# Head norms of q and k moved ahead of the gates' chain in a two-block transformer kernel

## The chip, the cores and the metric

The kernel runs on one core of one Trainium2 chip. The metric is device time in microseconds (us) of one execution. The core has five engines that work from queues of their own, each strictly in the order in which its instructions stand: TensorE (PE, with its weight loads PEld), VectorE (DVE), ScalarE (ACT), GpSimd (POOL) and SyncE (SP), which here only issues DMAs. They wait for each other through semaphores.

## The reference

256 tokens of width 1024 pass through two blocks in float32. The first block has a gated-delta layer and an HGRN2 layer. The second, where the change lies, is a mixer of three kinds of attention heads of width 64, followed by a feed-forward part:

```python
def _rms(x, g=None):                       # over one head's 64 columns
    xf = x.astype(jnp.float32)
    y = xf * lax.rsqrt(jnp.mean(xf * xf, axis=-1, keepdims=True) + EPS)
    return y if g is None else y * g.astype(jnp.float32)

def _mixer(hn, w_in, ...):
    proj = (hn @ w_in).astype(jnp.float32)
    fq, fk, fv, ff, mq, mk, mv, mi, mf, mo, bq, bk, bv = jnp.split(proj, idx, axis=-1)
    y_fox = _fox_attention(_rms(_to_heads(fq, 6), fox_q_g), _rms(_to_heads(fk, 6), fox_k_g),
                           _to_heads(fv, 6), ff + fox_f_bias)     # softmax with forget gates
    ...
    h_ml = _mlstm(mq, mk, mv, mi + ml_i_bias, mf + ml_f_bias)     # 4 heads with gates
    ...
    y_moba = _moba_attention(_rms(_to_heads(bq, 6), moba_q_g), _rms(_to_heads(bk, 6), moba_k_g),
                             _to_heads(bv, 6), slopes)            # softmax, 6 heads
    return concatenate([y_fox, y_ml, y_moba])
```

The "head norm" is `_rms` on the 24 q and k heads of the fox and moba kinds. The "gates" are `ff`, `mi` and `mf`: 14 columns per token, through a softplus and sums over the tokens.

## The kernel before

Every large product is made of three TensorE products of split float32 numbers (`hi*xh`, `hi*xl`, `lo*xh`). The weights come in one stream of 1 MB chunks; ACT casts each half chunk (`hi`), DVE forms the rest (`lo`, L206). Four half chunks of `hi` and `lo` have room, so a cast waits until TensorE has done with the half chunk four earlier. Results go to PSUM banks: four for the large products (tag `d`, in rows `psd`) and four for small ones (tag `m`, in rows `psm`), each used in turn and waited for by whoever needs it again.

The mixer (L1053) runs in this order on TensorE. `lstm_in` makes the mLSTM inputs and, beside the last of them, the gates' 16 columns. `heads` (L1139) then makes the q and k columns in three groups `g` of 512 columns, each for two halves `a_` of 128 tokens: 8 steps of 2 x 3 products, 48 products of 128x512 per group, in two `psd` banks. After each group two `head_norm` generators are queued. Then come the v columns in two groups of the same size (the `for g in range(2)` of `mixer`), then the output product.

Between the products small work is woven in. `Side` (L101) holds queues of generators; each has a width, the number of generators that may be under way. `side.tick(0.65)` after some products moves a planner's clock; a generator runs to its next `yield t` and is taken up again when the clock has moved by `t`. So the numbers behind `yield` are a plan, written as estimates, and they fix where TensorE's small products stand among the large ones: TensorE's instructions keep the order of the program. Those of ACT, DVE, POOL are put in order by a scheduler when the program is built. Three queues matter here:

- `gt`, width 1: `attention_gates`. After the softplus it makes `ag_cs` (sums over tokens, L1113), `ag_r` (L304), has TensorE transpose `ag_r`, copies and scans the result (`ag_rr`, `ag_mx`, L1126 and L1127), has it transposed back (`ag_mxc`), and sets `self.gated`.
- `kq`, width 2: `head_norm` (L1151). ACT squares the bank (`sq`), DVE sums 64 columns at a time (`hss`, L1158) and scales (L310), POOL raises to -1/2 (`hrs`, L321), DVE multiplies the bank by it (`sq`, L304), TensorE transposes four blocks into a `psm` bank, ACT and DVE copy them into `kq`. The multiplication is the last reader of the `psd` bank.
- `at`, width 4: `softmax_pair`, a pair of heads each. It waits for both norms of its group (pairs 0 and 1 need group 0, pairs 2 and 3 group 1, pairs 4 and 5 group 2). For each head of pairs 0 to 2 it takes a `psm` bank for the bias (two transposes of `ag_cs`) and one for the scores; heads of pairs 3 to 5 have their bias from POOL and take a score bank only. DVE frees them: two additions for the bias (with an ACT copy between them), two reductions for the scores (L1206, `pr`). All pairs are queued after the last q and k product.

Of the kernel before, what the change touches and what calls it, by code (L numbers as in the profile page):

```python
# [182 lines left out]
class Net:  # L183
# [966 lines left out]

    def head_norm(self, g, a_, b, kq):  # L1151
        nc, ep = self.nc, self.ep
        yield from self.wait(lambda: self.gated)
        sq = ep.tile([P, 512], F32, tag="sq", bufs=2, name=self.nm("sq"))
        ss, rs = (ep.tile([P, 8], F32, tag=n, bufs=2, name=self.nm(n)) for n in ("hss", "hrs"))
        v8 = lambda t: t.rearrange("p (h d) -> p h d", d=64)
        self.act(sq, b, AF.Square)
        nc.vector.tensor_reduce(ss, v8(sq), AX.X, ALU.add)  # L1158
        self.ts(ss, ss, 1.0 / 64, 1e-6)
        self.rsqrt(rs, ss)  # L1160
        self.tt(v8(sq), v8(b), rs.unsqueeze(2).to_broadcast([P, 8, 64]))
        yield 8.45
        t = self.ps("m")
        for j in range(4):
            self.tr(t[:, j * P:(j + 1) * P], sq[:, j * P:(j + 1) * P])
        s = slice(a_ * P, (a_ + 1) * P)
        for j in range(2):
            n = QK_BLOCKS[4 * g + j]
            self.act(kq[:, n, s], t[:, j * P:(j + 1) * P], AF.Copy, scale=self.gain[:, n // 3:n // 3 + 1])
        n = QK_BLOCKS[4 * g + 2]  # L1170
        m = QK_BLOCKS[4 * g + 3]
        nc.vector.tensor_copy(kq[:, n, s], t[:, 2 * P:3 * P])
        nc.vector.tensor_copy(kq[:, m, s], t[:, 3 * P:])
        self.kqdone.add((g, a_))
# [283 lines left out]
```

## Time and profile before

| what | us |
|---|---|
| median of 3 runs | 1015.01 (1011.16 to 1016.71) |
| the profiled execution | 1009.7 |
| its span in the trace | 1007.9 |
| TensorE busy | 979.7 (97%) |
| DVE busy | 757.2 (75%) |
| ACT busy | 555.2 (55%) |
| POOL busy | 51.2 (5%) |
| granted TensorE clock, mean | 0.998 |

The part that the change touches runs from 694.8 us (first q and k product) to 769.6 us (first product of the softmax weights with v). TensorE is busy nearly throughout; a busy share of TensorE counts the time in which it has a product under way, and its idle time is told with the engine it waited for. A row of the timeline gives the start, the duration, the engine, the line, the operation and its tiles, and in brackets the idle time of the engine before it.

### The profile page before, as it was taken

How to read it: one execution, taken by the hardware profiler on the slowest of the kernel's cores; microseconds unless marked ns; L12 is line 12 of the kernel's file. 1: busy time of each engine (PE TensorE's matmuls, PEld its weight loads, DVE VectorE, ACT ScalarE, POOL GpSimd, SP SyncE). 2: the span in 40 equal slices, each digit the busy share in tenths (PEclk: the TensorE clock that was granted, in tenths of full speed). 3: DMA queues.
4: the chain of work that ended last, by engine and by line, in shares of the span. 5: the costliest groups of instructions: out<-in, count | busy, mean ns of one | idle time of the engine just before them, and what ended most of it. 6: DMA issues, size and time to landing. Idle time of an engine off the chain costs nothing.

```text
span 1007.9 us, 19087 instructions
## 1 busy us (share of the span) xinstructions
PE 979.7 (97%) x7622; PEld 937.2 (93%) x7622; DVE 757.2 (75%) x1449; ACT 555.2 (55%) x1104; POOL 51.2 (5%) x59
## 2 busy tenths in 40 slices
PE   7999999999999999999999999899999999999998
PEld 5999989999998999998999999898867999999998
DVE  5788767878668978979697996879776787665543
ACT  6765556654544664464545544577566674444431
POOL 1000000000000000000000000000141000000000
PEclk9999999999999999999999999999999999999999
DMA  7445523345555685655556455354523257654560
GB/s 283 144 152 175 171 86 126 130 169 175 218 192 206 227 325 201 219 178 182 190 192 220 169 178 199 126 178 133 194 91 126 104 191 271 218 200 169 183 214 22
DMA packets 34617, 179.52 MB, mean 178 GB/s; under 512 B 7648, under 2 KB 8672, under 8 KB 16608
## 3 DMA queue, kind: packets, MB, share of 16 engines
q1 hardware_dynamic: 34096, 177.71, 49.9%
q8 instruction: 60, 0.98, 0.4%
q10 hardware_dynamic: 432, 0.59, 0.2%
q14 instruction: 29, 0.24, 0.1%
HBM read 176.97 MB, written 1.31 MB: 177 GB/s over the span
## 4 chain that ended last, share of the span: by engine, by line
PE 57%; DVE 7%; issue 4%; ACT 1%; POOL 1%; POOLq 0%; ACTq 0%; DVEq 0%
PE psd L294 49%; PE psm L294 6%; PE psm L297 2%; DVE lo L206 2%; DVE q L304 1%; ACT hi L206 1%; DVE xl L313 1%; DVE mt L313 0%; DVE wa L971 0%; DVE k L304 0%; DVE x L304 0%; DVE at L304 0%; DVE yl L217 0%; POOL hrs L321 0%; DVE lacc L313 0%
## 5 line engine op out<-in xcount | busy, mean ns | idle before, releaser
L206 DVE TENSOR_TENSOR lo<-raw,hi 128x1024 fp32r<-128x1024 f32 x280 | 341.2, 1222 | 132.4 <-ACT hi L206 130.2
L206 ACT CAST hi<-raw 128x1024 fp32r<-128x1024 f32 x280 | 292.9, 1047 | 249.1 <-PE psd L294 236.2
L294 PE MATMUL psd<-xh,hi 128*128 128x256 f32 (+1 forms) x1296 | 375.6, 290 | 0.0
L294 PE MATMUL psd<-xl,hi 128*128 128x256 f32 (+1 forms) x1296 | 366.8, 283 | 0.8 <-DVE xl L313 0.6
L294 PE MATMUL psd<-xh,lo 128*128 128x256 f32 (+1 forms) x1296 | 366.4, 283 | 0.2 <-DVE lo L206 0.2
L294 PEld LDWEIGHTS psd<-xl,hi 128*128 128x128 f32 x1296 | 245.7, 190 | 1.6 <-DVE xl L313 1.2
L294 PEld LDWEIGHTS psd<-xh,hi 128*128 128x128 f32 x1296 | 245.3, 189 | 1.0
L294 PEld LDWEIGHTS psd<-xh,lo 128*128 128x128 f32 x1296 | 245.5, 189 | 0.5 <-DVE lo L206 0.5
L294 PE MATMUL psd<-yh,hi 128*128 128x256 f32 x448 | 131.9, 294 | 3.7 <-ACT yh L216 3.7
L294 PE MATMUL psd<-yl,hi 128*128 128x256 f32 x448 | 127.1, 284 | 1.4 <-DVE yl L217 1.3
L294 PE MATMUL psd<-yh,lo 128*128 128x256 f32 x448 | 127.2, 284 | 0.0
L294 PEld LDWEIGHTS psd<-yh,hi 128*128 128x128 f32 x448 | 85.2, 190 | 5.2 <-ACT yh L216 4.3
L294 PEld LDWEIGHTS psd<-yl,hi 128*128 128x128 f32 x448 | 85.6, 191 | 2.4 <-DVE yl L217 2.4
L294 PEld LDWEIGHTS psd<-yh,lo 128*128 128x128 f32 x448 | 84.9, 189 | 0.1
L294 PE MATMUL psd<-hi,xh 128*128 128x512 f32 x144 | 59.0, 410 | 2.3 <-DVE sq L304 2.1
L971 DVE SCALAR_TENSOR_TENSOR wa<-wa,cr 128x1024 f32<-128x1024 f32 x48 | 58.4, 1218 | 2.8 <-ACT cr L316 1.6
L294 PE MATMUL psd<-hi,xl 128*128 128x512 f32 x144 | 56.9, 395 | 0.0
L294 PE MATMUL psd<-lo,xh 128*128 128x512 f32 x144 | 56.9, 395 | 0.0
L294 PE MATMUL psd<-al,hi 128*128 128x256 f32 x176 | 49.8, 283 | 0.0
L294 PE MATMUL psd<-ah,lo 128*128 128x256 f32 x176 | 49.7, 282 | 0.0
L294 PE MATMUL psd<-ah,hi 128*128 128x256 f32 x176 | 49.3, 280 | 0.0
L313 DVE SCALAR_TENSOR_TENSOR t<-psd,prm,t 128x255 f32<-128x255 f32 (+2 forms) x72 | 34.2, 476 | 3.9 <-ACT t L316 3.1
(330 smaller groups left out, 1381.9 us busy)
## 6 DMA issues: line engine op xcount, KB each, us to landing
raw<-in_w_dram SPq DMA_DIRECT2D x140, 1024.0 KB, 4.8
wa<-in_w_ada_dram SPq DMA_DIRECT2D x48, 512.0 KB, 4.8
cr<-in_c_dram SPq DMA_DIRECT2D x3, 512.0 KB, 6.0
out_dram<-fo SPq DMA_DIRECT2D x3, 256.0 KB, 2.1
cst<-in_cst_dram SPq DMA_DIRECT2D x1, 580.0 KB, 8.4
x<-in_xT_dram ACTq DMA_DIRECT2D x2, 256.0 KB, 4.4
x<-in_xT_dram SPq DMA_DIRECT2D x2, 256.0 KB, 5.0
lev<-in_lev_dram SPq DMA_DIRECT2D x1, 508.0 KB, 5.1
```

What stands on the lines that cost most here:

```text
L206: i = [nc.scalar.copy(hi, r), nc.vector.tensor_tensor(lo, r, hi.bitcast(F32), ALU.subtract)]
L294: self.nc.tensor.matmul(out, lhsT, rhs, start=start, stop=stop, skip_group_check=True, **k)
L297: self.nc.tensor.transpose(out, in_, self.c("ident")[:in_.shape[0], :in_.shape[0]])
L304: self.nc.vector.tensor_tensor(out, a, b, op)
L313: self.nc.vector.scalar_tensor_tensor(out, a, s, b, op0, op1)
L971: self.tc.keep_in_program_order(nc.vector.scalar_tensor_tensor(w, w, 1.0, c, ALU.mult, ALU.mult, accum_out=self.md(j)[:, i % 8:i % 8 + 1]))
```

## The change

In `head_norm` the wait for `self.gated` is moved from the first line to a place behind the multiplication, ahead of the transposes. The planner's delay between the multiplication and the transposes is 5.5 for one half of the tokens and 6.5 for the other, where it was 8.45 for both.

```diff
     def head_norm(self, g, a_, b, kq):
         nc, ep = self.nc, self.ep
-        yield from self.wait(lambda: self.gated)
         sq = ep.tile([P, 512], F32, tag="sq", bufs=2, name=self.nm("sq"))
...
         self.tt(v8(sq), v8(b), rs.unsqueeze(2).to_broadcast([P, 8, 64]))
-        yield 8.45
+        yield 5.5 + a_
+        yield from self.wait(lambda: self.gated)
         t = self.ps("m")
         for j in range(4):
             self.tr(t[:, j * P:(j + 1) * P], sq[:, j * P:(j + 1) * P])
```

What it does to the order shows at three places. The first is DVE at the norm of group 0, where the gates' chain runs too (`hss`, `hrs`, `sq` are the norm's; `ag_cs`, `ag_r` the gates').

```order
-L1158 TENSOR_REDUCE hss_8493<-sq_8492 128x8
-L1113 COPY ag_cs<-psm_8432 128x20
-L310 TENSOR_SCALAR hss_8493<-hss_8493 128x8
-L1158 TENSOR_REDUCE hss_8501<-sq_8500 128x8
+L1157 TENSOR_REDUCE hss_8424<-sq_8423 128x8
+L1157 TENSOR_REDUCE hss_8432<-sq_8431 128x8
+L310 TENSOR_SCALAR hss_8424<-hss_8424 128x8
+L1113 COPY ag_cs<-psm_8448 128x20
+L310 TENSOR_SCALAR hss_8432<-hss_8432 128x8
+L304 TENSOR_TENSOR sq_8423<-psd_8283,hrs_8425 128x512
+L304 TENSOR_TENSOR sq_8431<-psd_8284,hrs_8433 128x512
 L304 TENSOR_TENSOR ag_r<-ag_g,ag_cs 128x8
```

Both multiplications of the norm, each of which needs a result of POOL, now stand ahead of `ag_r`; before, `ag_r` stood ahead of both.

The second place is TensorE at the start of the v columns. Before, bias and score of two heads (the first of pairs 0 and 1) stood between the first products of v:

```order
L297 MATMUL psm_8640<-cst,ag_cs 128x128 x2
L294 MATMUL psm_8646<-kq_8282 128x128
L294 MATMUL psm_8646<-kq_8282 128x256
L297 MATMUL psm_8663<-cst,ag_cs 128x128 x2
L294 MATMUL psm_8669<-kq_8282 128x128
L294 MATMUL psm_8669<-kq_8282 128x256
L294 MATMUL psd_8625<-hi_8558,xh_7678 128x512
```

Now four heads stand there, the first of pairs 0 to 3; the fourth takes only a score bank:

```order
L297 MATMUL psm_8658<-cst,ag_cs 128x128 x2
L294 MATMUL psm_8664<-kq_8282 128x128
L294 MATMUL psm_8664<-kq_8282 128x256
L297 MATMUL psm_8681<-cst,ag_cs 128x128 x2
L294 MATMUL psm_8687<-kq_8282 128x128
L294 MATMUL psm_8687<-kq_8282 128x256
L297 MATMUL psm_8704<-cst,ag_cs 128x128 x2
L294 MATMUL psm_8710<-kq_8282 128x128
L294 MATMUL psm_8710<-kq_8282 128x256
L294 MATMUL psm_8728<-kq_8282 128x128
L294 MATMUL psm_8728<-kq_8282 128x256
L294 MATMUL psd_8643<-hi_8592,xh_7678 128x512
```

Three large products later the four second heads follow in the same way, with the banks 8764, 8770, 8787, 8793, 8810, 8816 and 8834. So 14 `psm` tiles stand around three large products where 8 stood. Group 1's norm is complete before all pairs are queued, and so pairs 2 and 3 start with pairs 0 and 1. Group 1's 8 transposes stand within group 2's products now.

The third place is DVE among those heads, where group 2's norm (`hss_8753`, `sq_8752`) now stands. Before, that norm's two multiplications stood among the scores of pairs 2 and 3:

```order
L304 TENSOR_TENSOR sq_8851<-psd_8520,hrs_8853 128x512
L308 TENSOR_SCALAR snm_8840<-smx_8839 128x1
L1209 RECIPROCAL ssm_8823<-ssm_8823 128x2
L304 TENSOR_TENSOR sq_8859<-psd_8521,hrs_8861 128x512
L308 TENSOR_SCALAR pr_8820<-pr_8820,ssm_8823 128x128
```

Now they stand among the scores of all four pairs:

```order
L1157 TENSOR_REDUCE hss_8753<-sq_8752 128x8
L308 TENSOR_SCALAR pr_8731<-pr_8731,ssm_8734 128x128
L1209 RECIPROCAL ssm_8716<-ssm_8716 128x2
L308 TENSOR_SCALAR pr_8731<-pr_8731,ssm_8734 128x256
L308 TENSOR_SCALAR pr_8713<-pr_8713,ssm_8716 128x128
L308 TENSOR_SCALAR pr_8713<-pr_8713,ssm_8716 128x256
L310 TENSOR_SCALAR hss_8753<-hss_8753 128x8
L304 TENSOR_TENSOR bias_8763<-psm_8764,cst 128x128
L304 TENSOR_TENSOR sq_8752<-psd_8539,hrs_8754 128x512
L304 TENSOR_TENSOR bias_8763<-psm_8764,cst 128x128
```

The multiplication `sq_8752`, which needs POOL's `hrs_8754`, stands between the two additions that free bank 8764.

## Rows read from the trace of the kernel before

**Rows 1.** The page: busy time and share of the span of each engine.

```profile
PE 979.7 (97%) x7622; PEld 937.2 (93%) x7622; DVE 757.2 (75%) x1449; ACT 555.2 (55%) x1104; POOL 51.2 (5%) x59
```

**Rows 2.** Waits of TensorE from 660 to 800 us: total, times, longest.

```profile
PE psd L294 <- DVE sq L304: 2.1, 1, 2.1
...
PE psm L297 <- DVE kq L1173: 0.3, 1, 0.3
```

**Rows 3.** Timeline of TensorE, 712 to 734 us (start, duration).

```profile
712.24 0.38 PE L297 MATMUL psm<-cst,ag_r 128*4 128x128 f32 x2
...
715.33 0.28 PE L297 MATMUL psm<-cst,ag_mx 4*128 4x4 f32 x2
...
730.93 0.40 PE L294 MATMUL psd<-lo,xh 128*128 128x512 f32 x1
733.42 0.47 PE L294 MATMUL psd<-hi,xh 128*128 128x512 f32 x1 [2.10 <-DVE sq L304]
```

**Rows 4.** Timeline of DVE, 710 to 717 us.

```profile
710.44 0.68 DVE L1158 TENSOR_REDUCE hss<-sq 128x8 f32<-128x512 f32 x1
711.04 0.17 DVE L1113 COPY ag_cs<-psm 128x20 f32<-128x20 f32 x1
711.15 0.17 DVE L310 TENSOR_SCALAR hss<-hss 128x8 f32<-128x8 f32 x1
...
711.83 0.16 DVE L304 TENSOR_TENSOR ag_r<-ag_g,ag_cs 128x8 f32<-128x8 f32 x1
...
713.08 0.69 DVE L304 TENSOR_TENSOR sq<-psd,hrs 128x512 f32<-128x512 f32 x1
713.68 0.40 DVE L1126 COPY ag_rr<-psm 4x256 f32<-4x256 f32 x1
```

**Rows 5.** Timeline of POOL, 705 to 752 us.

```profile
711.41 1.64 POOL L321 TENSOR_TENSOR hrs<-hss,mhalf 128x8 f32<-128x8 f32 x1 [32.37 <-DVE hss L310]
...
729.91 4.24 POOL L321 TENSOR_TENSOR hrs<-hss,mhalf 128x8 f32<-128x8 f32 x2 [13.68 <-DVE hss L310]
...
749.48 3.27 POOL L321 TENSOR_TENSOR hrs<-hss,mhalf 128x8 f32<-128x8 f32 x2 [7.23 <-DVE hss L310]
```

**Rows 6.** Timeline of ACT at the squares of group 0's norm.

```profile
709.17 1.07 ACT L316 ACTIVATE sq<-psd 128x512 f32<-128x512 f32 x2
```

**Rows 7.** DVE's instructions by form, 694 to 800 us: busy us, mean ns, idle before.

```profile
L206 DVE TENSOR_TENSOR lo<-raw,hi 128x1024 fp32r<-128x1024 f32 x25 | 30.6, 1223 | 12.8 <-ACT hi L206 11.3 <-PE psm L297 1.6
L1206 DVE CUSTOM_DVE_ANT_0 pr<-psm,bias 128x256 f32<-128x256 f32 x12 | 5.0, 414 | 0.0
L308 DVE TENSOR_SCALAR pr<-pr,ssm 128x256 f32<-128x256 f32 x12 | 4.4, 366 | 0.0
...
L308 DVE TENSOR_SCALAR pr<-pr,ssm 128x128 f32<-128x128 f32 x12 | 3.5, 291 | 0.1
L1206 DVE CUSTOM_DVE_ANT_0 pr<-psm,bias 128x128 f32<-128x128 f32 x12 | 3.4, 286 | 0.9 <-PE psm L294 0.7
L308 DVE TENSOR_SCALAR snm<-smx 128x1 f32<-128x1 f32 x24 | 3.3, 144 | 0.0
L304 DVE TENSOR_TENSOR bias<-psm,cst 128x128 f32<-128x128 f32 x12 | 3.2, 280 | 0.0
```

**Rows 8.** Timeline of TensorE at the first heads' bias and scores.

```profile
734.20 0.38 PE L297 MATMUL psm<-cst,ag_cs 128*128 128x128 f32 x2
734.51 0.92 PE L294 MATMUL psm<-kq 64*128 64x128 f32 x4
735.36 0.43 PE L297 MATMUL psm<-cst,ag_cs 128*128 128x128 f32 x2
```

**Rows 9.** Windows: busy us of each engine, then granted clock (PEclk), DMA share, GB/s.

```profile
640.00:645.00 5.00, 2.45 (x20) 2.04 (x18) 3.79 (x9) 2.93 (x5) 1.64 (x1) 1.00 0.49 195
645.00:650.00 5.00, 4.09 (x22) 3.90 (x23) 4.96 (x9) 3.94 (x9) 0.00 (x0) 0.73 0.60 205
650.00:655.00 5.00, 5.00 (x41) 5.00 (x41) 3.04 (x5) 4.14 (x6) 0.00 (x0) 0.92 0.03 8
...
730.00:735.00 5.00, 2.90 (x14) 2.00 (x13) 2.57 (x4) 1.04 (x1) 4.15 (x2) 1.00 0.23 98
735.00:740.00 5.00, 5.00 (x24) 2.98 (x24) 4.89 (x28) 3.04 (x14) 0.00 (x0) 1.00 0.62 210
```

## The prediction

> **What bounds the kernel now.** I read the busy shares first: TensorE is at work for 979.7 us, 97% of the span [rows 1], so only what makes it wait, or what adds to its work, moves the time. The change adds no product and removes none; it moves eight transposes and the heads' scores, and it moves work on DVE. So I asked next for TensorE's waits around the moved work, 660 to 800 us. Two of them belong to the head norm: 2.1 us where the first v product needs the bank that group 1's multiplication frees, and 0.3 us for a copy into `kq` [rows 2]. The timeline shows the first one: product at 730.93, next at 733.42 [rows 3]. Last I read, engine by engine, the two places where the new order differs: the gates' chain at 710 to 716 us [rows 3 to 6] and the start of the v columns [rows 7, 8].
>
> **What goes.** Group 1's norm can now run within group 2's products. It still does not start when its products end: the `kq` queue has width 2, and group 0's two norms leave it only after their transposes, which wait for the gates. But group 0's transposes now stand about 42 products earlier, group 1's multiplication frees its bank well ahead of the first v product, and its transposes stand within group 2, whose 48 products hide the chain of squares, sums, POOL and multiplication. I take the whole 2.1 us and the 0.3 us as gone: -2.4.
>
> **What comes first: the gates' chain waits behind POOL.** DVE works in order, and both multiplications of group 0's norm now stand ahead of `ag_r`. The squares cannot come sooner than they did: ACT starts them at 709.17 with no idle time before them [rows 6], in the same place of its order. So the first sum starts on DVE at 710.44 as before; a sum occupies DVE for 0.60 (710.44 to 711.04, for a duration of 0.68) [rows 4]. The second sum starts at 711.04 and the first scaling at 711.64. POOL starts 0.26 after a scaling's start (711.15 to 711.41) and DVE 0.03 after POOL's end (711.41 + 1.64 = 713.05, multiplication at 713.08) [rows 4, 5]. So POOL starts at 711.90 and does two powers one after the other. Two in a row took 3.27 us in one place and 4.24 in the other [rows 5]; I take 3.3, since in the 4.24 case a weight split ran on DVE beside them, and here DVE stands idle. POOL ends at 715.2; the second multiplication starts at 715.23, `ag_r` 0.60 later (713.08 to 713.68) at 715.83, done at 715.99, and TensorE transposes it about 0.1 later, 716.1. Before, `ag_r` started at 711.83 and the transposes at 712.24. TensorE has nothing else it may do: +3.9, between 3.6 (both powers at their shortest and no delay) and 4.9 (4.24 for the two). Behind the waiting multiplication on DVE also stands a `lo` split and the copy `ag_rr`; the split belongs to products half a group later, and the scan still ends inside the nine products between the two transposes (12.24 to 15.33 in rows 3, 3.1 us), so they cost nothing.
>
> [...]
>
> **What comes second: seven banks at a time.** At the start of the v columns TensorE now asks for 14 small tiles around three products, with four banks. A bank is free when DVE has read it, so DVE's pace sets the end. Up to bank 8810 (the bias of the last but one head) TensorE's own work is: three products at 0.23, three heads with bias at 1.16 (734.20 to 735.36), one without at 0.85 (734.51 to 735.36) [rows 8], three products, two heads at 1.16: 0.7 + 3.5 + 0.85 + 0.7 + 2.3 = 8.0 us from the end of group 2. DVE must by then have freed bank 8764 by the second addition to `bias_8763`. It starts late: the `lo` split ahead of the heads needs a cast that ACT begins only when group 2's products end, some 1.1 us later. From there it does, each at its duration less the 0.08 of overlap seen above: one split 1.14, seven bias additions 1.4, four short reductions 0.21 and four long ones 0.33 with eight readouts of 0.07, together 2.7, four scalings 0.21 and four 0.29, together 2.0, twelve small ones at 0.07, 0.9 [rows 7], one multiplication and one sum of the norm, 1.2, and a scaling, 0.1: 9.4 us. Then it stands still for POOL: 0.26 + 1.65 + 0.03, the multiplication 0.6 and the last addition 0.28: 2.8 us. 1.1 + 9.4 + 2.8 = 13.3 us against TensorE's 8.0: TensorE waits 5.3, if DVE never waits for ACT's exponentials. I take 5.5, between 4 (the split done earlier) and 7 (two or three round trips to ACT). Banks 8816 and 8834 need two more reductions and the third addition of `bias_8786`, behind one exponential: +1.0, between 0 and 1.5. The transposes of the softmax weights, 24 in a row where 12 stood, wait for ACT's copies out of four banks and for pairs 2 and 3, whose last scores are late now: +1.0, between 0 and 2.5.
>
> **The clock.** [...] At 730 to 735 it idled 2.1 us, and the clock stayed at 1.00 [rows 9]. Both new waits, 3.9 us and the chief one of the heads, are longer than the one that kept it. [...] I take 2.5 for both, between 0 and 3.5. [...]
>
> **Sum.** -2.4 + 3.9 + 5.5 + 1.0 + 1.0 + 2.5 = +11.5 us. On the profiled execution's own 1009.7 that is 1021.2. That execution lies 5.3 us below the median of the runs shown, 1015.0, whose lowest is 1011.2; I add the same difference to the median: 1026.5, rounded to 1026. All low ends together are -2.4 + 3.6 + 4 = +5.2, all high ends -2.4 + 4.9 + 7 + 1.5 + 2.5 + 3.5 = +17.0.
>
> **The rivals.** (a) *Only the gates' wait comes; the heads cost nothing.* For it: before, four heads with bias went by on two rounds without a wait of TensorE in rows 2, and in 735 to 740 us TensorE was busy for all 5.00 us [rows 9]. Against it: in the same 5 us DVE was busy for 4.89, so it had no room for seven tiles where four stood, and the power of POOL between two additions is a standstill that before did not stand there. Price: +3.9 - 2.4 = +1.5, to 1016.5, and 1018 with one fall of the clock.
>
> (b) *The head norm gets ahead of the gates, and only the gain is left.* The place is DVE at 710.44. If the multiplications were over when `ag_cs` is made, `ag_r` would not be late, and the sum would be -2.4, 1012.6: not slower. It decides at squares 3.9 us earlier than 709.17. Against it: ACT's order there is that of before, and it has no idle time ahead of the squares [rows 6]. For it only that group 0's products are complete some microseconds before the squares; the heads would have to be free too.
>
> (c) *The waits come, but the clock stays up.* Then the sum is +9.0, 1024. For it: the stretch of 730 to 735. It lies in the forecast's range.
>
> **How the numbers follow.** The forecast (gates' wait, heads' waits, gain; (c) included) has 0.83, with its own range +5 to +17, 1020 to 1032. (a) has 0.08, (b) 0.04, more than +17 0.05. What a measurement of this kernel can tell from no change is about 0.5%, 5 us. A median of a few runs moves by some 2 us (1011 to 1017 for single runs), so I widen the range to 1018 to 1033. Slower by over 0.5%: nearly all of the forecast and the 0.05: 0.87. Within 0.5%: (a), (b) and the forecast's lowest edge: 0.10. Faster by over 0.5% needs twice the whole gain and none of the waits: 0.03.
>
> **What would show it.** In the profile after, TensorE should wait once for about 3.9 us for DVE's `ag_r` near 712 us, with DVE idle before `sq` for POOL's `hrs`; the wait of 2.1 us for `sq` should be gone; from the start of the v columns there should be waits of `psm` tiles for DVE's `bias` and `pr` (one of 4 us or more, at 742 to 750 us), with DVE idle for POOL in it; and windows with a clock below 1.00 behind them. The first product of the softmax weights with v should start near 781, not 769.6. I am wrong if TensorE is not kept at `ag_r`, or if DVE frees seven tiles as fast as TensorE fills them.

## The result and the profile after

| | before | after |
|---|---|---|
| median | 1014.57 us (5 runs) | 1022.77 us |
| its runs | 1011.16 to 1016.71 | 1022.16 to 1024.4 |
| profiled execution | 1009.7 | 1022.41 |
| span in the trace | 1007.9 | 1020.6 |
| granted clock, mean | 0.998 | 0.991 |

The changed kernel is slower: the ratio is 1.0109, with a 95% interval of 1.0084 to 1.0134. One run of 4635.7 us, over four times as long as the others, is left out of the changed kernel's five. Profile against profile, the span is 12.7 us longer.

The page of the changed kernel has the same work on every engine as [rows 1], but for a busier TensorE:

```profile
PE 984.7 (96%) x7622; PEld 940.2 (92%) x7622; DVE 757.5 (74%) x1449; ACT 557.2 (55%) x1104; POOL 52.5 (5%) x59
```

The counts are those of before, and TensorE is busy for 5.0 us more: the same products took longer, which is a matter of the clock (the windows below). The other 7.7 us of the span are idle time. TensorE's waits between 660 and 815 us name it (total, times, longest); they answer to [rows 2]:

```profile
PE psm L297 <- DVE bias L304: 3.9, 1, 3.9
PE psm L297 <- DVE ag_r L304: 3.5, 1, 3.5
PE psm L297 <- DVE pr L308: 1.4, 1, 1.4
...
PE psm L294 <- DVE snm L308: 0.5, 1, 0.5
...
PE psm L297 <- ACT pts L1223: 0.2, 1, 0.2
```

The 2.1 us for `sq` and the 0.3 for `kq` are gone; 9.5 us stand in their place. The first new wait is at the gates. DVE and POOL there, to be laid beside [rows 4, 5]:

```profile
711.80 0.17 DVE L1113 COPY ag_cs<-psm 128x20 f32<-128x20 f32 x1
711.89 0.16 DVE L310 TENSOR_SCALAR hss<-hss 128x8 f32<-128x8 f32 x1
713.65 0.69 DVE L304 TENSOR_TENSOR sq<-psd,hrs 128x512 f32<-128x512 f32 x1 [1.59 <-POOL hrs L321]
715.25 0.69 DVE L304 TENSOR_TENSOR sq<-psd,hrs 128x512 f32<-128x512 f32 x1 [0.91 <-POOL hrs L321]
715.86 0.16 DVE L304 TENSOR_TENSOR ag_r<-ag_g,ag_cs 128x8 f32<-128x8 f32 x1
```

```profile
711.98 3.24 POOL L321 TENSOR_TENSOR hrs<-hss,mhalf 128x8 f32<-128x8 f32 x2 [32.85 <-DVE ag_cs L1113]
...
747.57 1.67 POOL L321 TENSOR_TENSOR hrs<-hss,mhalf 128x8 f32<-128x8 f32 x1 [5.02 <-DVE hss L310]
```

(The POOL row names `ag_cs`, which ended just before it; the power itself reads `hss`, which DVE scaled from 711.73 on.) `ag_cs` was there at 711.97, and `ag_r` needs nothing else that is late; it starts at 715.86 because two multiplications that wait for POOL stand ahead of it. TensorE's rows at that place and, below them, from the fifth head to the seventh (the third of the second round):

```profile
716.07 0.58 PE L297 MATMUL psm<-cst,ag_r 128*4 128x128 f32 x2 [3.52 <-DVE ag_r L304]
```

```profile
743.34 0.38 PE L297 MATMUL psm<-cst,ag_cs 128*128 128x128 f32 x2
744.19 0.92 PE L294 MATMUL psm<-kq 64*128 64x128 f32 x4 [0.47 <-DVE snm L308]
745.04 0.43 PE L297 MATMUL psm<-cst,ag_cs 128*128 128x128 f32 x2
745.40 0.92 PE L294 MATMUL psm<-kq 64*128 64x128 f32 x4
750.22 0.69 PE L297 MATMUL psm<-cst,ag_cs 128*128 128x128 f32 x2 [3.90 <-DVE bias L304]
```

The bank that is refilled at 750.22 is the one whose two bias additions DVE does at 747.33 and 749.88:

```profile
747.33 0.29 DVE L304 TENSOR_TENSOR bias<-psm,cst 128x128 f32<-128x128 f32 x1
749.27 0.69 DVE L304 TENSOR_TENSOR sq<-psd,hrs 128x512 f32<-128x512 f32 x1 [1.66 <-POOL hrs L321]
749.88 0.28 DVE L304 TENSOR_TENSOR bias<-psm,cst 128x128 f32<-128x128 f32 x1
```

Between them DVE stands still for 1.66 us, for POOL's power of 747.57. After that the windows (busy us of PE, PEld, DVE, ACT, POOL; granted clock; DMA share; GB/s), which answer to [rows 9]:

```profile
710.00:715.00 5.00, 2.55 (x12) 1.75 (x11) 2.75 (x7) 1.29 (x2) 3.02 (x2) 1.00 0.60 205
715.00:720.00 5.00, 3.93 (x12) 3.13 (x13) 4.12 (x6) 1.05 (x1) 0.21 (x1) 0.66 0.02 8
...
745.00:750.00 5.00, 1.32 (x7) 0.71 (x6) 3.33 (x13) 1.46 (x5) 1.67 (x1) 0.99 0.01 2
750.00:755.00 5.00, 4.78 (x13) 2.98 (x14) 3.81 (x23) 2.29 (x10) 2.35 (x2) 0.50 0.00 0
755.00:760.00 5.00, 5.00 (x19) 3.98 (x18) 1.23 (x1) 1.52 (x2) 0.00 (x0) 0.82 0.00 0
```

After both long waits the clock is below 1.00. In 750 to 755 TensorE was busy for 4.78 us at 0.50. Large products behind the heads start 0.43 us apart (754.56 and 754.99), where those ahead of the heads started 0.23 apart (736.76 and 736.99).

For every kernel of this study the stretch that matters can be cut at four marks of TensorE's timeline: the gates' sums (`sp_r`), the transposes of `ag_r`, the first head's bias (`ag_cs`), the first product of softmax weights and v. Times between the marks, in us, each from one profile:

| kernel | sums to `ag_r` | to first head | to weights x v | all |
|---|---|---|---|---|
| before | 2.75 | 21.96 | 35.37 | 60.08 |
| after | 6.50 | 22.07 | 44.14 | 72.71 |
| after, run again | 6.45 | 22.11 | 44.83 | 73.39 |
| group 0 without power | 3.24 | 21.37 | 44.37 | 68.98 |
| group 2 without power | 6.49 | 23.26 | 42.28 | 72.03 |
| pairs apart | 6.49 | 20.61 | 36.26 | 63.36 |
| filled wait | 6.49 | 20.62 | 44.75 | 71.86 |
| wait only | 6.45 | 20.52 | 46.45 | 73.42 |
| group 0 without power, pairs apart | 3.24 | 21.35 | 36.26 | 60.85 |
| delay only | 2.75 | 20.01 | 45.34 | 68.10 |
| late pairs only | 2.75 | 21.96 | 35.86 | 60.57 |
| delays only | 2.76 | 19.56 | 39.39 | 61.71 |
| shorter first delay | 2.76 | 19.56 | 35.53 | 57.85 |

Most values repeat from kernel to kernel: what an edit does at one place it does there alone. Where the second column differs with the same wait of about 3.5 us ahead of it (20.5 to 20.6, 22.1, 23.3), the clock behind that wait does (1.00, 0.66 or 0.67, and 0.51 at 715 to 720), as the experiments show. All but 0.1 us of the 12.7 us lie in this stretch (72.71 less 60.08 is 12.63).

### The profile page after: what moved, and what is told of

Same layout as the page of the kernel before. It is cut to its first block, busy times and chain, and to the rows that moved or that the text cites. A ratio compares the mean times of both kernels' runs of the same rounds, so it can differ in the third digit from the quotient of the medians.

```text
span 1020.6 us, 19094 instructions
## 1 busy us (share of the span) xinstructions
PE 984.7 (96%) x7622; PEld 940.2 (92%) x7622; DVE 757.5 (74%) x1449; ACT 557.2 (55%) x1104; POOL 52.5 (5%) x59
## 4 chain that ended last, share of the span: by engine, by line
PE 56%; DVE 7%; issue 4%; ACT 2%; POOL 1%; ACTq 0%; POOLq 0%; DVEq 0%
PE psd L294 48%; PE psm L294 6%; DVE lo L206 2%; PE psm L297 2%; ACT hi L206 1%; DVE q L304 1%; DVE xl L313 1%; POOL hrs L321 0%; DVE mt L313 0%; DVE wa L971 0%; DVE k L304 0%; DVE x L304 0%; DVE at L304 0%; DVE pr L1206 0%; DVE yl L217 0%
```

## The experiments

The experiments ran in three series, each on a chip of its own, with the kernel before beside them: medians 1011.3, 1011.03 and 1011.23 us. The changed kernel ran in the second of them; where a run is said to be so much less or more than the changed kernel, it is against that median, 1022.83. The intervals of the ratios are some 2 us either way, so medians less than 4 us apart are not told apart by the runs alone; there the sections of the table, from one profile each, decide.

**The changed kernel again.** No edit.

> The changed kernel itself, beside the runs that follow, so that they are compared on one chip. The waits of its profile are those of before to 0.1 us (3.5 at ag_r, 3.9 at bias, 1.4 at pr). Ratio to the kernel before 1.009 to 1.013. In pairs_apart a wait of 3.57 us at ag_r left the granted clock at 1.00, and in no_power_g2 the same wait of 3.57 took it to 0.81 and 0.51: if the fall after this wait is a matter of chance, the mean granted clock of the single runs here spreads (0.986 to 0.995) and the slower runs are those with the lower clock, about 1 us for each 0.001; if it belongs to the order of the work, all runs lie within 0.002 of each other.

1022.83 us, ratio 1.011 [1.0086, 1.0133]; waits 3.53, 3.89 and 1.36. The result holds in another series. The six runs have clocks of 0.988 to 0.991, the twenty of the kernel before 0.990 to 0.997: it is before that spreads (1009.02 us at 0.997, 1015.32 at 0.990), by about 0.9 us for each 0.001. The six clocks lie within 0.003 of each other, between the two outcomes that were named, so they do not say whether the fall behind the wait at `ag_r` is a matter of chance; both profiles of this kernel show it (0.66 and 0.67 at 715 to 720).

**Group 0's norm without POOL's power.** This asks what makes `ag_r` late.

```diff
-        self.rsqrt(rs, ss)
+        if g == 0:
+            rs = ss
+        else:
+            self.rsqrt(rs, ss)
```

> Group 0's norm leaves out POOL's power (its q and k are multiplied by the mean square itself); TensorE's order is that of the changed kernel. The theory (TensorE waits at ag_r because DVE stands behind two powers of POOL, 3.24 us): ag_r on DVE at about 712.5 instead of 715.86, the wait of 3.5 us before its transposes falls below 0.8. Part comes back at the transposes of ag_mx, since a weight split and the second multiplication now stand ahead of the copy ag_rr: a wait of 0.5 to 1.5 there. No idle time of over 2 us at 710 to 720 us, so the granted clock of 715 to 720 is 1.00 and not 0.66 (1.7 us more). Sum: 3 to 5 us shorter than the changed kernel, first product of the softmax weights with v near 778 instead of 781.9. Rival 1 (the time is given back at the heads, which end when DVE is done whatever comes before): ag_r early, but the same total within 1 us. Rival 2 (ag_r is late because of the sums, not of POOL): wait stays at 3 us or more.

1019.15 us, 3.7 less than the changed kernel (ratio to before 1.0067 [1.0045, 1.0089]). TensorE's two rows:

```profile
712.23 0.38 PE L297 MATMUL psm<-cst,ag_r 128*4 128x128 f32 x2 [0.32 <-DVE ag_r L304]
716.08 0.28 PE L297 MATMUL psm<-cst,ag_mx 4*128 4x4 f32 x2 [0.66 <-DVE ag_mx L1127]
```

`ag_r` starts at 712.02 on DVE. The wait falls from 3.52 to 0.32 and 0.66 comes back at `ag_mx`; the heads' section is unchanged (44.37 against 44.14). So POOL's two powers make the wait, and nothing of it is given back at the heads: both rivals fall.

**Group 2's norm without POOL's power.** The same edit with `g == 2`.

> The same for group 2 alone: its norm leaves out POOL's two powers; TensorE's order is that of the changed kernel. The theory (of the chief wait of the heads, 3.9 us at bias of the seventh head, the standstill of DVE for POOL, 1.66 us, is a part, and DVE's own pace the rest): that wait falls to about 2.2 us, the clock's fall behind it gets smaller; 1.5 to 3 us shorter than the changed kernel. Rival 1 (DVE's pace and ACT's round trips alone set the end, the standstill lies beside something else): no change, within 0.5 us. Rival 2 (POOL is the whole cause): wait under 0.5 us, 4 to 6 us shorter.

1021.39 us, 1.4 less than the changed kernel, a little under the range expected. The heads' rows that answer to those above:

```profile
740.32 0.43 PE L297 MATMUL psm<-cst,ag_cs 128*128 128x128 f32 x2 [0.69 <-DVE snm L308]
...
743.83 0.92 PE L294 MATMUL psm<-kq 64*128 64x128 f32 x4 [0.46 <-DVE snm L308]
...
747.72 0.69 PE L297 MATMUL psm<-cst,ag_cs 128*128 128x128 f32 x2 [1.76 <-DVE snm L308]
```

Together 2.91 us where 4.37 stood: the standstill for POOL (1.66) is a part, and two thirds of the wait are DVE's own pace. Both rivals fall. The heads' section is 1.9 us shorter, but the whole stretch only 0.7 (72.03 against 72.71), because after the wait at `ag_r` the clock fell further in this execution (0.81 at 710 to 715 and 0.51 at 715 to 720; 23.26 in the second column).

**Pairs apart.** Takes seven of fourteen banks out of the burst.

```diff
         yield from self.wait(lambda: {(p_ // 2, 0), (p_ // 2, 1)} <= self.kqdone)
+        if p_ in (2, 3):
+            yield 5.0
```

> The changed kernel with pairs 2 and 3 held back by 5.0 of the planner's clock, so that four tiles with bias stand at the start of v and pairs 2 and 3 come 21 products later, about as before the change; the gates' place is left alone. The theory (seven banks at a time keep TensorE waiting for DVE): the wait of 3.9 us for bias and the two of 0.5 and 1.4 behind it go, new ones at the heads of pairs 2 and 3 and at the softmax weights are 1 to 3 in all, and the clock stays up at 750 to 760; the wait of 3.5 at ag_r stays. 4 to 6 us shorter than the changed kernel, 1017 to 1019. Rival (only the wait at ag_r costs, the heads' waits lie beside something that ends no sooner): no change within 1 us.

1013.79 us, 9.0 less than the changed kernel; ratio to before 1.0025 [1.0006, 1.0044]. More than expected. The waits fell as thought: 1.6 in four pieces at the softmax weights remain in the heads' section where 6.0 stood, 4.4 less. The rest is the clock, which stays up at both places:

```profile
710.00:715.00 5.00, 1.43 (x8) 0.86 (x7) 2.50 (x7) 0.00 (x0) 3.24 (x2) 1.00 0.49 195
715.00:720.00 5.00, 5.00 (x28) 3.95 (x27) 3.31 (x7) 2.91 (x6) 0.00 (x0) 1.00 0.27 82
...
750.00:755.00 5.00, 4.39 (x25) 3.35 (x26) 4.06 (x27) 4.16 (x17) 2.34 (x2) 1.00 0.40 164
```

That the clock stays up at 715 to 720 is no work of the edit, which stands 20 us later; the 1.5 us of the second column (20.61 against 22.07) are not its gain. In the kernel with group 2 changed, the wait at `ag_r` was just as long (3.57), and its windows read:

```profile
710.00:715.00 5.00, 1.43 (x6) 0.89 (x5) 2.58 (x5) 0.00 (x0) 3.08 (x2) 0.81 0.43 180
715.00:720.00 5.00, 5.00 (x14) 3.45 (x14) 2.27 (x5) 1.04 (x1) 0.00 (x0) 0.51 0.25 54
```

**Filled wait.** Gives TensorE 16 products that nothing needs in place of half the wait.

```diff
+        for k in range(16):
+            self.mm(t[:, :T], self.xh[:, k % KT, :P], self.xl[:, k % KT, :T])
         for a_ in range(2):
             self.tr(t[:4, a_ * P:(a_ + 1) * P], self.r[:, a_])
```

> The changed kernel with 16 products of 128x256 (xh by xl, result overwritten) put ahead of the transposes of ag_r, into the same bank: they fill some 1.9 us of the 3.5 us in which TensorE idles and delay nothing. The theory (the fall of the clock at 715 to 720 comes from TensorE's idle time): idle 1.6 us instead of 3.5, the granted clock of that window 0.9 to 1.00 and not 0.66, 1 to 1.7 us shorter than the changed kernel. Rival (the clock's fall costs nothing, since DVE's chain of the gates, copy, scan, is what ends last there): clock up, but total the same within 0.3 us. Rival 2: clock falls all the same, total the same.

1021.05 us, 1.8 less (1.0079 [1.0057, 1.0102]). The wait is 1.68 us, `ag_r` comes no sooner (6.49 in the first column), the clock of 715 to 720 is 1.00, and the second column is 20.62, not 22.07. With the fall to 0.66 or 0.67 this column is 22.07 and 22.11, without a fall 20.61, 20.62 and 20.52: the fall cost 1.45 us, and that it cost nothing is refuted. The heads' section came out 0.6 longer in this profile, so the stretch gained 0.85. That busy work takes the fall away is likely but not shown: with the whole wait left in, two of five profiles read 1.00 too. The clocks of the six runs, 0.991 to 0.994 against 0.988 to 0.991 for the changed kernel run again, point that way.

**Wait only.** The move without the shorter delay.

```diff
-        yield 5.5 + a_
+        yield 8.45
         yield from self.wait(lambda: self.gated)
```

> The changed kernel with the delay behind the multiplication left at 8.45, as before the change: only the wait for the gates is moved. TensorE still has 4 heads, 3 products, 4 heads. If the move alone brings both waits (the theory): 3.5 at ag_r and a chief wait of the heads of 4 to 6 (both multiplications of group 2 stand among the heads, two powers of POOL one after the other), within 2 us of the changed kernel or up to 3 slower. If the shorter delay is what brings the heads together (rival): no wait over 1 us at the heads, 4 us or more shorter than the changed kernel.

1024.59 us, 1.8 more than the changed kernel (1.0126 [1.01, 1.0151]). The waits are 3.48 at `ag_r` and 5.39 at the seventh head, where DVE stands still for POOL twice, 0.84 and 1.62:

```profile
746.00 0.69 DVE L304 TENSOR_TENSOR sq<-psd,hrs 128x512 f32<-128x512 f32 x1 [0.84 <-POOL hrs L321]
...
746.67 0.28 DVE L304 TENSOR_TENSOR bias<-psm,cst 128x128 f32<-128x128 f32 x1
748.58 0.69 DVE L304 TENSOR_TENSOR sq<-psd,hrs 128x512 f32<-128x512 f32 x1 [1.62 <-POOL hrs L321]
749.19 0.28 DVE L304 TENSOR_TENSOR bias<-psm,cst 128x128 f32<-128x128 f32 x1
```

The move alone brings both waits; with the shorter delay the heads' wait is 3.90, not 5.39. The 1.8 us between the two medians are not clear of their spread.

**Delay only.** The other half: the kernel before with the delay `5.5 + a_`.

> The other half of the edit alone: the kernel before (wait for the gates ahead of the squares) with the delay 5.5 and 6.5. In TensorE's order the heads come in three rounds, pairs 0 and 1 at the start of v, their second heads 3 products later, pairs 2 and 3 after 6 more, with the transposes of group 1's second norm between. The theory (the move of the wait brings ag_r late and, with the short delay or without it, puts eight heads around three products): no wait at ag_r, that for sq of 2.1 us gone or below 1, since group 0's norms leave the queue about 15 products earlier, heads' waits 2 to 5 in several pieces: 0 to 4 us longer than the kernel before and 7 us or more shorter than the changed one. Rival (the delay carries part of the changed kernel's loss): one wait of 3.5 or more, the clock falls, 6 us or more longer than the kernel before.

1019.41 us, ratio 1.0075 [1.0055, 1.0095]: a miss. The waits came as expected:

```profile
PE psm L297 <- DVE bias L304: 2.3, 1, 2.3
PE psm L294 <- DVE bias L304: 0.6, 1, 0.6
...
PE psm L294 <- DVE kq L1173: 0.5, 1, 0.5
```

With 0.4 in two more pieces that is 3.8 us where 2.4 stood, and none at `ag_r`. But the clock fell behind them, and longer than in the changed kernel:

```profile
740.00:745.00 5.00, 2.74 (x12) 1.79 (x11) 3.25 (x18) 1.38 (x7) 2.65 (x2) 0.89 0.21 88
745.00:750.00 5.00, 4.15 (x12) 2.45 (x10) 3.73 (x20) 3.53 (x12) 0.61 (x2) 0.50 0.01 2
750.00:755.00 5.00, 5.00 (x15) 3.40 (x14) 3.85 (x18) 2.12 (x9) 4.43 (x3) 0.50 0.00 0
755.00:760.00 5.00, 5.00 (x18) 4.00 (x19) 1.30 (x4) 1.05 (x1) 0.00 (x0) 0.74 0.00 0
```

1.4 us of waits more became 8.0 us in the last column of the table: 5 x (0.11 + 0.50 + 0.50 + 0.26) = 6.9 us of TensorE's work at most were lost to the clock. So the delay carries a loss of its own, as the rival had it, by the clock rather than by a long wait.

**Both cures.** Group 0 without power, and pairs apart: the two diffs above together.

> Both cures at once: pairs 2 and 3 held back by 5.0, and group 0's norm without POOL's power (its q and k are multiplied by the mean square itself). If the two waits are the whole loss, what is left is the gain: the wait of 2.1 us for sq is gone, against it stand 0.3 at ag_r, 0.7 at ag_mx and about 1.6 at the softmax weights; no fall of the clock; 0 to 2 us shorter than the kernel before. Rival (something else in the change costs too, such as transposes of group 1 within group 2's products): 2 us or more longer than the kernel before.

1010.67 us, ratio 0.999 [0.9974, 1.0007]. Every section is the sum of the single edits (3.24, 21.35, 36.26), and the whole loss is gone: no third cause is needed. The gain of 2.4 us is eaten by waits of 0.3, 0.7 and 1.6.

**Shorter first delay**, a version to beat both. On the kernel before:

```diff
-        yield 8.45
+        yield (6 + a_ if g == 0 else 9.5)
...
         yield from self.wait(lambda: {(p_ // 2, 0), (p_ // 2, 1)} <= self.kqdone)
+        if p_ in (2, 3):
+            yield 6
```

> A version made to beat both: the kernel before (the wait for the gates stays ahead of the squares, so ag_r keeps its place), with the delay 6 and 7 for group 0 and 9.5 for groups 1 and 2, so that group 0's norms leave the queue earlier and group 1's begins within group 2's products; pairs 2 and 3 are held back by 6, so that four heads with bias come at the start of v and pairs 2 and 3 about 45 products later. The theory: no wait at ag_r, none for sq (2.1 us gone), heads' waits below 1 us in all: 1.5 to 3.5 us shorter than the kernel before. Rival (the wait for sq stands beside something as late): within 1 us of the kernel before.

1007.36 us, ratio 0.9949 [0.9931, 0.9968]: faster than both. TensorE's waits from 660 to 815 us:

```profile
PE psd L294 <- DVE xl L313: 0.6, 1, 0.6
PE psm L297 <- DVE x L304: 0.4, 1, 0.4
PE psm L297 <- DVE snm L308: 0.2, 1, 0.2
```

The first two belong to later work. In the profile the stretch is 2.23 us shorter (57.85 against 60.08), the wait for `sq` and no more. The medians lie 3.7 apart and the ratio says about 5, more than expected: the clocks of the nine runs lie at 0.995 to 0.998, where 9 of the 20 runs of the kernel before lie at 0.993 or less. That the wait for `sq` sometimes brings the clock down would fit; no profile here caught it, and the rest of the gain stays unexplained.

**Its two edits alone.** Pairs 2 and 3 held back by 6 with the delays of before; and the delays 6, 7 and 9.5 with the pairs of before.

> One of the two edits of shorter_first_delay alone, on the kernel before: pairs 2 and 3 held back by 6, delays as before. If the gain of 5 us of shorter_first_delay comes from the norm of group 1 getting its place within group 2 (the theory), the wait for sq of 2.1 us is still there and the time is that of the kernel before, within 1.5 us. Rival (the gain is that of fewer heads together): 3 us or more shorter than the kernel before, with the wait for sq.

1010.53 us, ratio 1.0005 [0.9988, 1.0023], with the wait of 2.11 for `sq`. Its profiled execution is one of the longer ones (1012.4 us at a clock of 0.993), and it does not show the clock falling behind that wait. At 730 to 740, around the wait, the clock is 1.00. It is 0.66 at 130 to 135, far ahead of the stretch, where the profile of the kernel before reads 1.00:

```profile
130.00:135.00 5.00, 4.66 (x26) 4.50 (x26) 2.05 (x10) 3.15 (x10) 1.01 (x1) 0.66 0.27 111
...
735.00:740.00 5.00, 4.37 (x21) 2.85 (x22) 4.09 (x16) 1.01 (x5) 1.36 (x1) 1.00 0.15 34
```

So at least part of what parts the runs of one kernel lies far from the change.

> The other edit of shorter_first_delay alone: the delays 6, 7 and 9.5, pairs 2 and 3 not held back, so that they come 3 products after the transposes of group 1, right behind pairs 0 and 1. The theory (a gain needs both, since the earlier norm by itself draws the pairs forward into DVE's busiest stretch): the wait for sq is gone, against it 2 to 5 us of waits at bias and pr of pairs 2 and 3: between 1 us shorter and 3 us longer than the kernel before. Rival (the heads have room enough in three rounds): 3 us or more shorter.

1011.78 us, ratio 1.0 [0.9984, 1.0016]: no wait for `sq` (19.56 in the second column), against it 3.1 us at `kq`, `bias` and the softmax weights, with the clock at 1.00. All twelve clocks are at 0.995 or more here, without the wait for `sq`; of the 12 runs of "late pairs only", which has it, 3 are at 0.993 or less. That speaks for the wait, but does not show it. Neither half gains; the earlier norm is worth its 2.4 us only with the heads held apart.

## Why the prediction was right

The forecast was a loss of 11.5 us on the profiled execution, for four reasons and against one gain. It measured 12.6 in this stretch, and the first product of the softmax weights with v started at 782.28 (near 781 predicted). Step by step, all from the two profiles:

| term | predicted | measured |
|---|---|---|
| waits for `sq` and `kq` gone | -2.4 | -2.4 |
| gates' wait behind two powers | +3.9 | +3.75 |
| heads up to bank 8810 | +5.5 | +4.4 (0.47 + 3.90) |
| banks 8816 and 8834 | +1.0 | 0 |
| softmax weights' transposes | +1.0 | +1.6 (0.24 + 1.35) |
| clock | +2.5 | +5.3 (what is left of 12.6) |

That the sum came so close is partly luck: the clock was 2.8 too low, and the three terms of the heads together 1.5 too high (7.5 against 6.0).

- *The gates' wait* was right in its mechanism and to 0.15 us: POOL's pair took 3.24 with DVE idle beside it (3.3 taken), and `ag_r` started at 715.86 (715.83 predicted). The run without the power shows the cause. The choice of 3.3 and not 4.24 for the pair held as well: in this profile a single power took 1.67 with DVE standing still (747.57), and 2.62, 2.52 and 2.62 where a `lo` split of 1.23 ran on DVE beside it (726.52, 730.81, 738.68). That the split makes the power longer was the author's estimate; no run takes the split away.
- *The heads* were right in place and mechanism: one chief wait, at bank 8810, at 750.22, with DVE standing still for POOL between the two additions. From group 2's end (737.45) to 750.22 are 12.8 us, where the sum had 13.3. What was too high is the tail: banks 8816 and 8834 cost nothing. Behind the chief wait TensorE ran at half its clock (0.50 at 750 to 755), which would give DVE time to catch up; that this is the reason is not shown, since all five profiles with that wait have a window of 0.50 behind it.
- *The clock* was the term that was mis-sized. No run shows the term of 2.5. It was the author's estimate for two falls, from the one fall of before: its windows of 0.73 and 0.92 [rows 9] give 5 x (0.27 + 0.08) = 1.75 for one, so 3.5 for two, of which a part was taken to be hidden. In its place the runs showed 1.45 and 3.5 to 3.8. The first fall cost 1.45 (filled wait against the changed kernel). The second cost 3.5 to 3.8, by subtraction only, since no run fills that wait. The heads' section grew by 8.77, of which 5.7 are waits (6.0 less 0.3), and 0.75 us of transposes had left it (20.61 in "pairs apart" against 21.96 less 2.1): 3.8. Against "pairs apart" it is 7.88 longer, of which 4.4 are waits: 3.5. The windows allow 5 x (0.01 + 0.50 + 0.18) = 3.45 us at most, so some tenths of the 3.8 belong to something else. Little of the fall was hidden, since the wait ended just as the clock fell: the window of 750 to 755 is 0.50 with TensorE busy for 4.78. The price of 1.75 came from one profile. By the same reckoning the place it was read from, 640 to 655 us, lost twice as much in the profile after, 5 x (0.09 + 0.50 + 0.09) = 3.4, behind the same wait of 2.3 us for `yh`; one fall was too small a sample.
- *The step to the median* was off the other way. The profiled execution lay 5.3 us below the median before; after, it lies 0.4 below (1022.41 and 1022.77). So 1026 was 3 too high, though the loss was larger than the sum. The clocks of the single runs of before spread from 0.990 to 0.998 in the three series, those of the changed kernel from 0.986 to 0.991; both profiles of the changed kernel have the fall at the heads, and how its other runs fare there is not shown.
- *Rival (a)*, that the heads cost nothing, falls by "pairs apart": their burst cost 7.9 us (44.14 against 36.26), more than the gates. *Rival (b)* needed squares 3.9 us earlier than 709.17; ACT started them at 709.27. *Rival (c)*, that the clock stays up, falls for the heads in every profile that had the chief wait (0.50 in a window behind it in all five); behind the gates' wait it held in two profiles of five.

## What to carry to other kernels

An instruction that needs a slow engine's result holds up everything queued behind it: here two multiplications that waited 1.59 and 0.91 us for POOL kept `ag_r` from 711.97 to 715.86. Before work is moved earlier on an in-order engine, look for the short chain behind it that TensorE is waiting for. Work that becomes ready earlier also releases its followers earlier: hold the followers where there was room for them, as the version that gained did (0.2 us of waits at the heads, where the changed kernel has 6.0). Count the clock as a term of its own for each wait, from the same kernel's windows; it can be dearer than the wait, as in "delay only" (1.4 us more of waits, 8.0 us in the stretch), and one fall seen once is a poor price for it.

## What was not expected of the hardware

- The length of one wait did not decide whether the clock falls. The wait at `ag_r` of 3.5 us left the window behind it at 1.00 twice (3.57 in "pairs apart", 3.48 in "wait only"), and took it to 0.66, 0.67 and 0.51 three times (3.52, 3.53, 3.57). In "delay only" a longest wait of 2.26 was followed by 0.50 in two windows; in "delays only" 3.1 us in pieces of at most 0.7 left it at 1.00. What decides it is not shown: why one wait was followed by a fall and another of the same length was not stays open.
- Run times of one kernel follow the mean granted clock: before, 1009.02 us at 0.997 and 1015.32 at 0.990. A difference of a few microseconds between two medians is read with their clocks beside them.
